# A hybrid attention and linear-attention step on one core: how far VectorE, ScalarE and GpSimd run in written order through layer 1

## The chip, the cores and the metric

The kernel runs on one core of a Trainium2 chip. The metric is the device time of one execution in microseconds (us). Before the change the median of three runs is 2579.01 us, from 2577.28 to 2580.81.

## What is computed

The reference runs two layers on 512 prompt rows and on 8 sequences of 16 sample rows, 640 rows in all, with a model width of 2048, in float32. Layer 0 is stick-breaking attention. Layer 1, where the change lies, is gated linear attention (GLA). Cut to what matters here:

```python
shift, scale, gate = jnp.split(c @ w_ada[i] + b_ada[i], 3, axis=-1)
h = rmsnorm(x, norm_g[i]) * (1 + scale[:, None]) + shift[:, None]
...
q, k, v, r, a_lr = jnp.split(h @ w_in, [nk, 2 * nk, 2 * nk + nv, 2 * nk + 2 * nv], axis=-1)
g = (jax.nn.log_sigmoid((a_lr @ w_a2 + b_a).astype(f32)) / GLA_TAU).reshape(B, T, GLA_HEADS, GLA_DK)
...
S, o = lax.scan(gla_chunk, S0, (to_chunks(q), to_chunks(k), to_chunks(v), to_chunks(g)))
...
y = (o.reshape(B, T, nv) * jax.nn.silu(r.astype(f32))).astype(h.dtype) @ w_out
```

The product `h @ w_in` gives queries, keys, values and gates for four heads, and `w_a2` is a small matrix (16 rows) that the decay gate needs later.

## The kernel before

**Numbers in two parts.** TensorE multiplies in a rounded float32 form, so each operand is held as a high part and a low part. `halves` (lines 133 to 135) makes them: ScalarE rounds the operand (line 134, CAST, named `wh` for weights), and VectorE subtracts that from the operand (line 135, `wl`). `split` (line 139) does so for a piece of weights of 128 x 1024. The buffers for the parts of a weight piece come in a ring of three, two in the pool `wp` and every third one in a pool that is given for the time being (`ring3`).

**Seven products.** Most of `h @ w_in` of layer 1 is done in blocks of 256 columns by a scheme with seven products in place of eight (`by_sevens`, line 480). A block is called a job here. Each of its products, named P0 to P6 below, is 24 matmuls (line 541) of a 128 x 128 weight tile with 320 rows. The seven weight pieces of a job, W0 to W6 in the order of the products, are made from four quarters that are loaded (b11, b12 and b22 into the buffers `wb`, b21 into a buffer `wr`), by `weights` (line 499):

- W0 is b11 itself. Behind it VectorE makes t = b22 - b12 (line 507) and b12 - b11 (line 508).
- W1 is b11 + t (made by line 510). W2 is b21, and behind it b21 - b11 is made (line 513).
- W3 is t. W4, W5 and W6 are b12 - b11, b21 - b11 and b22.

`ready` (line 528) keeps three pieces ahead: at the start of product Pn the piece for two products later is split, ahead of Pn's own matmuls in the program. Where a product ends, ScalarE or VectorE takes its sum out of PSUM (lines 547, 554 and 561: the tiles `m`, `u` and `out`). `u` of P1 must be taken before P3 goes on in the same bank, and `u` of P3 before P5 does.

**Seventeen jobs.** Three hold keys and queries, six hold values (`keep_value`, line 1329), eight hold gates (`keep_gate`, line 1340: a sigmoid on ScalarE, line 1346, and a product on VectorE, line 1348, per half). A finished job of values is turned into rows while the next job runs: `as_rows` (line 613) transposes it on TensorE in three groups g0, g1 and g2 (line 623) as a side lane, which `Side` (line 270) starts by a count of TensorE time. After each group `halves` writes a high and a low part of `kr` out of PSUM, and SyncE stores each to the DRAM tensors `gv`. There is one buffer for the high part of `kr` and one for the low part, so that a group's conversion waits until the store of the group before it is done.

**What sets the order.** TensorE always runs in the order in which the program is written. The other engines' instructions are put in order by a scheduler that goes by its own times, except inside a `manual_schedule` block, where the named engines too run in written order. One such block (`in_order`, line 1245) opens at layer 0's output projection. It closes at line 1365, when the last sum of layer 1's activations (`adds`, line 1270) is made. SyncE, which issues the loads (line 71) and stores (line 74) here, stays with the scheduler. On the chip each engine works through its list from front to back.

**Around the place of the change.** Ahead of it, two plain products make the queries of head 0 (`queries`, line 1311, matmuls on line 596, their copies `pl` on line 1304 and their stores `gq`). `next(sevens)` at the 30th step of the queries makes W0, t and b12 - b11 of the first job. Then the pool `om` is closed, and six small loads bring `w_a2` (`wa2r`), ScalarE rounds it (line 1374), VectorE subtracts (line 1375) and SyncE stores the result (`wa_d`), which only the next stage reads. Then `drive(sevens)` (line 1377) runs all seventeen jobs, `side.finish()` what is left of the side lanes, and `h2.again` (line 1380) makes activation parts for the stage that follows.

Of the kernel before, what the change touches and what calls it, by code (L numbers as in the profile page):

```python
# [41 lines left out]
def hybrid_step_kernel(ctx: ExitStack, tc: tile.TileContext, A: dict, O: list):  # L42
# [296 lines left out]
    def drive(*gens):  # L339
        for g in gens:  # L340
            for _ in g:
                side.tick()
# [812 lines left out]
    with tc.tile_pool(name="o0", bufs=1, reuse_waits="tile") as po, ExitStack() as only_d:  # L1155
# [89 lines left out]
        in_order = ExitStack()  # L1245
# [116 lines left out]
                next(sevens)  # L1362
        for _ in adds:
            pass
        in_order.close()
        more.close()
        ring3["n"] = 2
        ring3["pool"] = only_d.enter_context(tc.tile_pool(name="w2", bufs=1, reuse_waits="tile"))
# [7 lines left out]
        store(wa2_d, wa2.bitcast(F32))  # L1376
        drive(sevens)
        side.finish()
        ring3["pool"] = None
        h2.again(1, wq)  # L1380
    s1_pool.close()
# [541 lines left out]
```

## Time and profile before

| what | value |
|---|---|
| median of three runs | 2579.01 us |
| profiled execution, its own time | 2576.39 us |
| span of the profiled execution | 2574.6 us |
| TensorE (PE) busy | 2444.2 us, 95% of the span |
| VectorE (DVE) busy | 1604.6 us, 62% |
| ScalarE (ACT) busy | 1019.7 us, 40% |
| GpSimd (POOL) busy | 231.4 us, 9% |
| mean granted TensorE clock | 0.979 of full speed |
| the seven products of layer 1 | 1622 to 2059 us of the span |

The profile is of one execution, which took 2576.39 us: 1.8 us beside its span, and 2.6 us under the median. PE stands for TensorE's matmuls, PEld for its weight loads, SPq, ACTq and POOLq for the queues that issue DMAs. In rows of the timeline stand the start, the duration, the engine, the line, the operation with its output and inputs, and in brackets how long the engine had been idle and what released it. A row with x2 or more holds several instructions.

### The profile page before, as it was taken

How to read it: one execution, taken by the hardware profiler on the slowest of the kernel's cores; microseconds unless marked ns; L12 is line 12 of the kernel's file. 1: busy time of each engine (PE TensorE's matmuls, PEld its weight loads, DVE VectorE, ACT ScalarE, POOL GpSimd, SP SyncE). 2: the span in 40 equal slices, each digit the busy share in tenths (PEclk: the TensorE clock that was granted, in tenths of full speed). 3: DMA queues.
4: the chain of work that ended last, by engine and by line, in shares of the span. 5: the costliest groups of instructions: out<-in, count | busy, mean ns of one | idle time of the engine just before them, and what ended most of it. 6: DMA issues, size and time to landing. Idle time of an engine off the chain costs nothing. (4 is left out here: it accounts for less than half of the span.)

```text
span 2574.6 us, 43617 instructions
## 1 busy us (share of the span) xinstructions
PE 2444.2 (95%) x17321; PEld 2147.2 (83%) x17321; DVE 1604.6 (62%) x2445; ACT 1019.7 (40%) x1820; POOL 231.4 (9%) x489
## 2 busy tenths in 40 slices
PE   6899999999999999999999979899999998989998
PEld 4589999989999988787777758899999997766776
DVE  4675655555566656666776665766666655666466
ACT  4342222222223335655443344333333364565133
POOL 1220000000000000000000050000000114334200
PEclk8899999999999999999999989999999999999999
DMA  9966666766663366666665853344444367777464
GB/s 337 320 212 218 217 204 219 228 216 192 207 199 118 116 209 207 228 213 222 214 226 170 252 188 123 88 114 130 126 124 118 112 221 249 240 250 230 164 230 148
DMA packets 452797, 502.05 MB, mean 195 GB/s; under 512 B 26090, under 2 KB 349810, under 8 KB 452466
## 3 DMA queue, kind: packets, MB, share of 16 engines
q1 hardware_dynamic: 433090, 442.11, 54.1%
q0 software_dynamic: 16048, 51.92, 6.0%
q10 hardware_dynamic: 3456, 5.24, 0.6%
q8 instruction: 136, 2.23, 0.4%
q14 instruction: 67, 0.55, 0.1%
HBM read 410.05 MB, written 89.13 MB: 194 GB/s over the span
## 5 line engine op out<-in xcount | busy, mean ns | idle before, releaser
L541 PE MATMUL ps_mm<-sums,wh 128*128 128x320 f32 x2880 | 644.0, 312 | 2.2 <-ACT wh L134 2.2
L541 PEld LDWEIGHTS ps_mm<-sums,wh 128*128 128x128 f32 x2880 | 481.2, 189 | 11.3 <-issue 7.4
L541 PE MATMUL ps_mm<-h,wh 128*128 128x320 f32 x2160 | 484.7, 312 | 5.7 <-DVE u L547 3.2
L541 PE MATMUL ps_mm<-sums,wl 128*128 128x320 f32 x1440 | 446.4, 310 | 1.5 <-DVE wl L135 1.5
L541 PEld LDWEIGHTS ps_mm<-h,wh 128*128 128x128 f32 x2160 | 360.3, 188 | 22.1 <-issue 14.5
L135 DVE TENSOR_TENSOR wl<-wr,wh 128x1024 fp32r<-128x1024 f32 x192 | 236.0, 1230 | 213.9 <-ACT wh L134 213.1
L134 ACT CAST wh<-wb 128x1024 fp32r<-128x1024 f32 x178 | 186.8, 1049 | 449.6 <-PE ps_mm L541 381.6
L541 PE MATMUL ps_mm<-h,wl 128*128 128x320 f32 x1080 | 334.5, 310 | 0.7 <-DVE wl L135 0.7
L134 ACT CAST wh<-wr 128x1024 fp32r<-128x1024 f32 x192 | 201.6, 1050 | 316.0 <-PE ps_mm L541 194.1
L541 PEld LDWEIGHTS ps_mm<-sums,wl 128*128 128x128 f32 x1440 | 271.6, 189 | 2.0 <-DVE wl L135 2.0
L135 DVE TENSOR_TENSOR wl<-wb,wh 128x1024 fp32r<-128x1024 f32 x178 | 217.6, 1222 | 63.0 <-ACT wh L134 62.5
L642 PE MATMUL ps_mm<-wh,ogh 128*128 128x512 f32 x460 | 201.8, 439 | 13.2 <-ACT ogh L134 7.5
L596 PE MATMUL ps_mm<-h,wh 128*128 128x320 f32 x896 | 208.0, 319 | 6.1 <-ACT wh L134 3.3
L541 PEld LDWEIGHTS ps_mm<-h,wl 128*128 128x128 f32 x1080 | 203.5, 188 | 1.0 <-DVE wl L135 1.0
L642 PE MATMUL ps_mm<-wh,ogl 128*128 128x512 f32 x460 | 182.8, 397 | 0.6 <-DVE ogl L135 0.4
L642 PE MATMUL ps_mm<-wl,ogh 128*128 128x512 f32 x460 | 182.1, 396 | 0.0
L596 PEld LDWEIGHTS ps_mm<-h,wh 128*128 128x128 f32 x896 | 151.1, 191 | 17.6 <-issue 7.0
L596 PE MATMUL ps_mm<-h,wl 128*128 128x320 f32 x448 | 139.9, 312 | 3.1 <-DVE wl L135 3.1
L642 PEld LDWEIGHTS ps_mm<-wh,ogh 128*128 128x128 f32 x460 | 87.9, 191 | 41.5 <-issue 14.8
L898 DVE TENSOR_TENSOR_SCAN k<-k,zero_c 128x544 f32<-128x544 f32 (+4 forms) x96 | 93.3, 976 | 29.6 <-ACT k L894 16.9
L470 PE MATMUL ps_mm<-wh,h 128*128 128x512 f32 x288 | 101.7, 418 | 6.8 <-ACT h L134 4.9
L642 PEld LDWEIGHTS ps_mm<-wh,ogl 128*128 128x128 f32 x460 | 87.4, 190 | 21.8 <-DVE ogl L135 1.8
(341 smaller groups left out, 3830.6 us busy)
## 6 DMA issues: line engine op xcount, KB each, us to landing
ar<-in_w_ada_dram SPq DMA_DIRECT2D x160, 512.0 KB
wb<-in_sb_w_in_dram SPq DMA_DIRECT2D x82, 512.0 KB
kc<-in_cache_sb_k_dram SPq DMA_DIRECT2D x64, 512.0 KB
vc<-in_cache_sb_v_dram SPq DMA_DIRECT2D x64, 512.0 KB
wb<-in_gla_w_in_dram SPq DMA_DIRECT2D x51, 512.0 KB
wr<-in_gla_w_in_dram SPq DMA_DIRECT2D x45, 512.0 KB
wr<-in_sb_w_in_dram SPq DMA_DIRECT2D x44, 512.0 KB
ar<-in_w_ada_dram SPq DMA_DIRECT2D x64, 256.0 KB
```

Of the source, the lines that this page charges most:

```text
L134: nc.scalar.copy(hi, x)
L135: dve.tensor_tensor(lo, x, hi.bitcast(F32), op=ALU.subtract)
L470: mm(acc[a], l, by(l, r[:, e, :]), start=j == 0 and e == 0 and first, stop=j == 7 and e == 1 and last)
L541: mm(acc, l[:, k, :], by(l[:, k, :], r), start=start and k == 0 and first, stop=k == 7 and last, skip_group_check=True)
L596: mm(acc[nt], l[:, k, :], by(l[:, k, :], r), start=k0 == 8 and k == 0 and first, stop=k0 == 0 and k == 7 and last)
L642: mm(acc, l, by(l, r[:, e, :]), start=i == 0 and e == 0 and first, stop=i == 1 and e == 1 and last)
L898: dve.tensor_tensor_scan(kr, kr, zeros[:, :w], 1.0, ALU.mult, ALU.add)
```

## The change

The end of the `in_order` block moves from ahead of the loads of `w_a2` to behind `side.finish()`. VectorE, ScalarE and GpSimd now run in written order through the conversion of `w_a2` and all seventeen jobs.

```diff
         for _ in adds:
             pass
-        in_order.close()
         more.close()
         ring3["n"] = 2
         ring3["pool"] = only_d.enter_context(tc.tile_pool(name="w2", bufs=1, reuse_waits="tile"))
...
         store(wa2_d, wa2.bitcast(F32))
         drive(sevens)
         side.finish()
+        in_order.close()
         ring3["pool"] = None
         h2.again(1, wq)
```

No instruction is added or removed. TensorE's order is the same in both kernels, GpSimd's differs only in six DMAs and conversions of the next stage, and the other engines' lists differ as follows.

ScalarE at the start of the first job. The names: `wh<-wb` is the rounding of W0 and then of W1, `wh<-wr` that of W2, `pl` the last copy of the queries, `wa` the rounding of `w_a2`.

```order
 L134 CAST sums<-sx 128x320 x2
 L134 CAST wh<-wb 128x1024
-L134 CAST wh<-wr 128x1024
 L1304 COPY pl<-ps_mm 128x320
-L134 CAST wh<-wb 128x1024
-L1374 CAST wa_17021<-wa2r 96x1024
+L1373 CAST wa_17020<-wa2r 96x1024
+L134 CAST wh<-wb 128x1024
+L134 CAST wh<-wr 128x1024
```

W2 went from ahead of the copy to behind W1, and the rounding of `w_a2` from behind W1 to ahead of it.

VectorE at the same place. `wl` is the low part of W0, then of W2 (`wr`) and W1 (`wb`); L507, L508, L510 and L513 are the sums of weight quarters.

```order
 L135 TENSOR_TENSOR wl<-wb,wh 128x1024
 L507 TENSOR_TENSOR t_17001<-wb 128x1024
-L135 TENSOR_TENSOR wl<-wr,wh 128x1024
-L508 TENSOR_TENSOR wb<-wb 128x1024
+L508 TENSOR_TENSOR wb<-wb 128x1024
+L1374 TENSOR_TENSOR wa_17020<-wa2r,wa_17020 32x1024
 L510 TENSOR_TENSOR wb<-t_17001,wb 128x1024
-L513 TENSOR_TENSOR wr<-wr,wb 128x1024
-L135 TENSOR_TENSOR wl<-wb,wh 128x1024
-L1375 TENSOR_TENSOR wa_17021<-wa2r,wa_17021 32x1024
+L135 TENSOR_TENSOR wl<-wb,wh 128x1024
+L135 TENSOR_TENSOR wl<-wr,wh 128x1024
```

The subtraction for `w_a2` (line 1375 before, 1374 now) now stands ahead of L510, which makes W1.

VectorE in a job that runs while the values of the job before it are turned into rows, before the change, from W3's low part (`wl<-t`) on; the three rows of `kr` are g0, g1 and g2, the two of `u` are the sums of P1 and P3.

```order
L135 TENSOR_TENSOR wl<-t_18130,wh 128x1024
L135 TENSOR_TENSOR kr<-ps_tp,kr 128x512
L547 TENSOR_TENSOR u<-ps_mm,m_18190 128x320
L135 TENSOR_TENSOR wl<-wb,wh 128x1024
L135 TENSOR_TENSOR kr<-ps_tp,kr 128x512
L135 TENSOR_TENSOR wl<-wr,wh 128x1024
L135 TENSOR_TENSOR kr<-ps_tp,kr 128x256
L507 TENSOR_TENSOR t_18384<-wb 128x1024
L547 TENSOR_TENSOR u<-ps_mm,m_18190 128x320
```

The same place in the changed kernel, from L513 on.

```order
L513 TENSOR_TENSOR wr<-wr,wb 128x1024
L135 TENSOR_TENSOR kr<-ps_tp,kr 128x512
L135 TENSOR_TENSOR wl<-t_18129,wh 128x1024
L135 TENSOR_TENSOR kr<-ps_tp,kr 128x512
L547 TENSOR_TENSOR u<-ps_mm,m_18189 128x320
L135 TENSOR_TENSOR kr<-ps_tp,kr 128x256
L135 TENSOR_TENSOR wl<-wb,wh 128x1024
L135 TENSOR_TENSOR wl<-wr,wh 128x1024
L547 TENSOR_TENSOR u<-ps_mm,m_18189 128x320
```

All three groups of `kr` now stand ahead of W4 (`wl<-wb`), g1 also ahead of the `u` of P1, and the t of the next job (L507) has gone to behind W0 of that job. ScalarE's list has the same pattern. On SyncE the load of b12 now stands between g0's two stores and the load of b21 behind them; before, b12 came ahead of both, b21 between them, and b22 ahead of g1's second store.

## The prediction

> **What bounds the kernel now.** I read the page first, then the windows of the stretch that the change reorders, then what TensorE waited for in it, and last the timelines of the engines at its start and in one job.
>
> The page's first line, and the windows view: time of each engine within a stretch of layer 1's seven products, with the granted clock behind POOL.
>
> ```profile
> span 2574.6 us, 43617 instructions
> ...
> 1620.00:1740.00 120.00, 115.50 (x764) 114.60 (x764) 77.45 (x81) 41.00 (x51) 0.00 (x0) 0.97 0.40 112
> 1740.00:1880.00 140.00, 137.06 (x939) 135.56 (x939) 90.11 (x102) 49.85 (x65) 0.00 (x0) 1.00 0.46 130
> 1880.00:2060.00 180.00, 179.32 (x1223) 179.09 (x1222) 124.69 (x136) 69.20 (x85) 7.58 (x20) 1.00 0.40 115
> ```
>
> TensorE is busy for 115.50 of 120 us, 137.06 of 140 and 179.32 of 180, VectorE for some two thirds of each. So TensorE is the bound, and an order of the other engines can win little more here than TensorE's idle time: 4.5, 2.9 and 0.7 us. It can lose more, by making TensorE wait. The waits view of TensorE over 1620 to 2095 us (total, times, longest) names what there is:
>
> ```profile
> PE ps_mm L541 <- ACT wh L134: 3.0, 2, 2.3
> PE ps_mm L541 <- DVE u L547: 2.7, 4, 0.9
> ```
>
> The first is at the start of the first job, the second in the jobs that turn values into rows.
>
> **The start of the first job.** TensorE's timeline around product P0, then ScalarE's, VectorE's and SyncE's.
>
> ```profile
> 1619.80 0.31 PE L596 MATMUL ps_mm<-h,wl 128*128 128x320 f32 x1
> 1622.42 0.56 PE L541 MATMUL ps_mm<-h,wh 128*128 128x320 f32 x2 [2.31 <-ACT wh L134]
> ...
> 1628.39 0.31 PE L541 MATMUL ps_mm<-h,wl 128*128 128x320 f32 x1
> 1629.42 0.55 PE L541 MATMUL ps_mm<-sums,wh 128*128 128x320 f32 x2 [0.72 <-ACT wh L134]
> ```
> ```profile
> 1621.32 1.05 ACT L134 CAST wh<-wb 128x1024 fp32r<-128x1024 f32 x1
> 1622.27 1.05 ACT L134 CAST wh<-wr 128x1024 fp32r<-128x1024 f32 x1
> 1623.21 0.42 ACT L1304 COPY pl<-ps_mm 128x320 f32<-128x320 f32 x1
> 1628.32 1.05 ACT L134 CAST wh<-wb 128x1024 fp32r<-128x1024 f32 x1 [4.69 <-DVE wb L510]
> 1630.66 1.05 ACT L1374 CAST wa<-wa2r 96x1024 fp32r<-96x1024 f32 x1 [1.29 <-DMA wa2r<-in_gla_w_a_dram]
> ```
> ```profile
> 1624.67 1.22 DVE L135 TENSOR_TENSOR wl<-wr,wh 128x1024 fp32r<-128x1024 f32 x1
> 1625.81 1.22 DVE L508 TENSOR_TENSOR wb<-wb 128x1024 f32<-128x1024 f32 x1
> 1627.06 1.23 DVE L510 TENSOR_TENSOR wb<-t,wb 128x1024 f32<-128x1024 f32 x1
> ...
> 1631.74 1.22 DVE L1375 TENSOR_TENSOR wa<-wa2r,wa 32x1024 fp32r<-32x1024 f32 x1 [1.06 <-ACT wa L1374]
> ```
> ```profile
> 1606.73 17.26 SPq L74 DMA_DIRECT2D gq<-pl  x2
> 1625.98 2.65 SPq L71 DMA_DIRECT2D wa2r<-in_gla_w_a_dram  x6
> ```
>
> P0 ends at 1628.70 (1628.39 + 0.31). P1 begins at 1629.42, 1.10 after ScalarE took up W1 (1628.32), which came 0.03 behind L510 (1627.06 + 1.23). ScalarE met the small loads `wa2r` at 1630.66, and they were what it waited for: they had landed just then. That wait held up nothing, since W1 stood ahead of it. Now it stands ahead of W1 on both engines, and behind it are queued L510, W1, W2 and L513, for which P1 and P2 wait.
>
> Step by step. The copy `pl` moves up one CAST, from 1623.21 to 1622.26 (its sums were done at 1620.11), and with it the second store of `gq`. SyncE's loads of `wa2r` come behind it; I move them by the same 0.95, from 1625.98 to 1625.03, and their landing from 1630.66 to 1629.71. The CAST of `w_a2` takes 1.05, to 1630.76. The subtraction starts at 1630.79, and L510 follows 1.14 later (as L508 followed `wl`, 1624.67 to 1625.81), at 1631.93, and ends at 1633.16. W1 is taken up at 1633.19 and P1 begins 1.10 later, at 1634.29, against 1629.42: **+4.9 us**. TensorE stands still for 5.6 us, and nothing else is in its list there. If the loads land no earlier than before, it is +5.8. The last of the six is issued 2.65 behind the first, at 1627.7, so that they cannot land 2 us sooner than I have them: not below +2.9.
>
> P1 also meets the clock. The same windows view, with the clock behind POOL's 0.00:
>
> ```profile
> 1624.50:1628.00 3.50, 3.50 (x17) 3.50 (x16) 3.47 (x4) 0.00 (x0) 0.00 (x0) 0.54 0.43 142
> 1628.00:1631.40 3.40, 1.92 (x10) 1.40 (x10) 2.65 (x3) 1.79 (x2) 0.00 (x0) 0.97 0.29 65
> 1631.50:1635.00 3.50, 3.50 (x16) 3.50 (x15) 2.44 (x2) 1.47 (x3) 0.00 (x0) 0.52 0.88 239
> ```
>
> Behind each idle spell some 3.5 us run at half clock, which costs 1.7 us; behind the half-idle stretch 1628.0 to 1631.4 it is already paid once. I expect one such stretch for P1 as before, so 0, from -0.4 (part of it falls into the longer pause) to +1.7 (two of them). The Trainium skill, TensorE: Matmul & The Clock Gate, section "What's actually happening", says that after an idle window of about 3.4 us the array runs at half clock until it has been busy for such a window. By it the longer pause is followed by a half-clock stretch of its own, and if the window in which P1 starts again is not counted as busy the sum is 1.7 us higher. The clock of 0.52 behind the stretch that was idle for under half of it shows that less than a whole idle window is enough here.
>
> **The six jobs beside which values are turned into rows.** Their length now: the start of P5 in the last job before them and in the last of them; two sums of P1 one plain job apart; and the transposes of g0 and g2 in one job.
>
> ```profile
> 1720.09 0.46 PE L541 MATMUL ps_mm<-h,wh 128*128 128x320 f32 x2
> ...
> 1878.81 0.54 PE L541 MATMUL ps_mm<-h,wh 128*128 128x320 f32 x2 [0.87 <-DVE u L547]
> ```
> ```profile
> 1660.52 0.49 DVE L547 TENSOR_TENSOR u<-ps_mm,m 128x320 f32<-128x320 f32 x1 [1.38 <-PE ps_mm L541]
> 1685.16 0.49 DVE L547 TENSOR_TENSOR u<-ps_mm,m 128x320 f32<-128x320 f32 x1 [1.38 <-PE ps_mm L541]
> ```
> ```profile
> 1756.96 0.60 PE L623 MATMUL ps_tp<-ident,out 128*128 128x128 f32 x4
> 1761.36 0.38 PE L623 MATMUL ps_tp<-ident,out 128*128 128x128 f32 x2
> ```
>
> A plain job takes 24.64 us, so a product 3.52. From g0 to g2 lie one product and eight transposes, 4.40 us: 0.88 for eight, 1.10 for a job's ten. Six jobs without a wait would take 6 x 25.74 = 154.4; they took 158.7. So 4.3 us are lost now (a little over the idle 2.9, since a matmul's modelled end hides the first part of a gap), at P5, which waits for the `u` of P3 behind g2 and t. By the new order that wait goes (t stands behind W0). What is late next shows in the conversions and stores of one job:
>
> ```profile
> 1758.34 0.59 ACT L134 CAST kr<-ps_tp 128x512 fp32r<-128x512 f32 x1
> 1762.38 0.59 ACT L134 CAST kr<-ps_tp 128x512 fp32r<-128x512 f32 x1 [3.45 <-DMA gv<-kr]
> ```
> ```profile
> 1759.29 0.68 DVE L135 TENSOR_TENSOR kr<-ps_tp,kr 128x512 fp32r<-128x512 f32 x1
> 1765.51 0.69 DVE L135 TENSOR_TENSOR kr<-ps_tp,kr 128x512 fp32r<-128x512 f32 x1 [0.33 <-DMA gv<-kr]
> 1771.07 0.43 DVE L135 TENSOR_TENSOR kr<-ps_tp,kr 128x256 fp32r<-128x256 f32 x1 [2.13 <-DMA gv<-kr]
> ```
> ```profile
> 1758.95 0.37 SPq L74 DMA_DIRECT2D gv<-kr  x1
> 1759.41 0.42 SPq L71 DMA_DIRECT2D wr<-in_gla_w_in_dram  x1
> 1760.00 3.35 SPq L74 DMA_DIRECT2D gv<-kr  x2
> ```
>
> A store with no load just ahead of it frees its buffer in 3.4 us (1758.95 to 1762.38); one 0.6 us behind a 512 KB load takes 5.5 (1760.00 to 1765.51). In the new order, on this job's clock: g0's low part is stored at 1759.25, 0.4 behind the load of b12, so g1's low part begins at about 1764.6, ends at 1765.3, and the `u` of P1 at 1765.8. P2 begins 0.22 after g2, at 1761.58, and P3 would begin at 1765.10: 0.85 late. g1's high part (1762.3) is stored behind the load of b21, so g2's can be written at 1767.6; ScalarE takes up W4 behind it, at 1767.9, and VectorE, behind g2's low part, ends W4 at 1770.2. P4 begins at 1769.5 and asks for the low part 0.3 later: 0.5 late. With loads in the queue ending half a microsecond sooner the two come to 1.0, so I take 1.2 per job, 7.2 for six, against 4.3 now: **+2.9 us**. Were both stores free in 3.4 us, no wait would be left, and the term is -4.3. A low store took at most 6.7 us in these jobs (issue and next use):
>
> ```profile
> 1865.65 3.32 SPq L74 DMA_DIRECT2D gv<-kr  x2
> ...
> 1872.32 0.69 DVE L135 TENSOR_TENSOR kr<-ps_tp,kr 128x512 fp32r<-128x512 f32 x1 [1.55 <-DMA gv<-kr]
> ```
>
> With that at both places a job loses 2.4, and the term is +10.
>
> **The rest.** The three jobs of keys and queries and the eight of gates have no stores in the way of a conversion. Each piece is split two products (7.0 us) ahead, and CAST and subtraction take 2.3; VectorE's load is 124.69 of 180 us. Even with t, L508 and L510 in one turn (3 x 1.23) a piece is ready in time: 0. At the end the first gate half's product goes behind the last sum, so its store is some 2 us later and the last upper activation parts 0.5 to 1 later, while TensorE has other products: +0.3. Behind 2095 us a few conversions change places by one, each 1.05 to 1.23 long: 0, within 2 either way.
>
> **Sum.** 4.9 + 0 + 2.9 + 0 + 0.3 = 8.1 us on the profiled execution's 2576.39, so 2584.5; the median of the runs lies 2.6 above it, and on its 2579.0 I forecast **2587 us**.
>
> **Rivals.**
>
> - *The stores decide the other way.* If the engines take the stores ahead of the loads' remainder, the buffers are free in 3.4 us and the 4.3 us of waits go: 4.9 - 4.3 + 0.3, 2580. For it speaks that SyncE issues g0's high store ahead of the load now; against, the 5.5 us of each store directly behind a load. Chance 0.16.
> - *The small loads are early* (the side where it is not slower). If `wa2r` lands by 1625.9, the end of an L508 that has moved up by one subtraction, its conversion fills that subtraction's place (1.14) and P1 begins where it did: 0 at the start, and with the -4.3 of free stores and 0.3, 2575. It decides at 3.8 us sooner than my 1629.71. Against it stands the first issue at 1625.98. Chance 0.05, mostly short of 0.2%.
> - *Late stores pile up.* W4 late in every value job, +10 there, and a second half-clock stretch: 4.9 + 1.7 + 10, 2596. For it speaks the 6.7 us store; against, that it was one of six. Chance 0.09.
> - *The forecast*, 2584 to 2592: chance 0.70.
>
> **Numbers.** A measurement of this kernel can tell about 0.2% (5.2 us) from no change. Slower by more: the forecast, the piled-up case and the upper part of the first rival, 0.79. Within it 0.18, faster 0.03. The range runs from 2580.5, a little over the free stores, to 2595, short of the piled-up case; it leaves out under 2 in 10.
>
> **What would show it.** In the profile of the changed kernel: P1's first matmul at 1634 with over 5 us idle, released by ScalarE's `wh`; the CAST of `w_a2` at 1629.7 ahead of W1's; no wait of P5 for `u` in the value jobs, but one of P3 for `u` and of P4 for `wl`; none in the gate jobs. The prediction is wrong if P1 begins within 2 us of 1629.4, or if the six value jobs take under 154.5 or over 165 us.

## The result, and the profile after

The changed kernel takes 2588.54 us (median of 20 runs, 2580.16 to 2593.11), the kernel before 2578.93 (20 runs, 2574.48 to 2583.93). The ratio is 1.0034, with a 95% interval from 1.0026 to 1.0042: slower by 6.7 to 10.8 us. The profiled execution of the changed kernel took 2580.16 us, the lowest of its runs, so that its stages are compared with those of the kernel before, and not its total.

The page's first line and the windows view over the stretch of the seven products:

```profile
span 2578.4 us, 43568 instructions
...
1620.00:1740.00 120.00, 111.49 (x744) 110.55 (x745) 73.36 (x74) 37.65 (x45) 0.00 (x0) 0.97 0.38 105
1740.00:1880.00 140.00, 135.32 (x928) 133.83 (x927) 88.13 (x100) 49.00 (x65) 0.00 (x0) 1.00 0.47 132
1880.00:2065.00 185.00, 184.32 (x1257) 184.09 (x1256) 128.55 (x139) 70.81 (x87) 8.16 (x21) 1.00 0.40 116
```

The page counts 49 instructions fewer than before; they are semaphore instructions, and each engine's own count of work is the same. TensorE is now idle for 8.5 us in the first of these stretches (4.5 before), for 4.7 in the second (2.9) and for 0.7 in the third (0.7). The waits view of TensorE from 1615 to 2062 us (total, times, longest) says for what:

```profile
PE ps_mm L541 <- ACT wh L134: 9.5, 2, 7.2
PE ps_mm L541 <- DVE u L547: 4.7, 6, 1.8
PE ps_mm L541 <- DVE wl L135: 1.1, 2, 0.7
```

The first row has grown from 3.0 to 9.5 and the second from 2.7 to 4.7. These are the two places of the prediction.

**The start of the first job**, in the timelines of TensorE, ScalarE, VectorE and SyncE:

```profile
1620.30 0.56 PE L541 MATMUL ps_mm<-h,wh 128*128 128x320 f32 x2 [2.31 <-ACT wh L134]
1621.56 0.42 PE L541 MATMUL ps_mm<-h,wl 128*128 128x320 f32 x1 [0.70 <-DVE wl L135]
1632.20 0.90 PE L541 MATMUL ps_mm<-sums,wh 128*128 128x320 f32 x2 [7.15 <-ACT wh L134]
1633.46 0.64 PE L541 MATMUL ps_mm<-sums,wl 128*128 128x320 f32 x1 [0.36 <-DVE wl L135]
```
```profile
1620.15 0.42 ACT L1304 COPY pl<-ps_mm 128x320 f32<-128x320 f32 x1
1627.52 1.04 ACT L1373 CAST wa<-wa2r 96x1024 fp32r<-96x1024 f32 x1 [6.95 <-DMA wa2r<-in_gla_w_a_dram]
1631.11 1.04 ACT L134 CAST wh<-wb 128x1024 fp32r<-128x1024 f32 x1 [2.54 <-DVE wb L510]
```
```profile
1622.67 1.22 DVE L508 TENSOR_TENSOR wb<-wb 128x1024 f32<-128x1024 f32 x1
1628.60 1.22 DVE L1374 TENSOR_TENSOR wa<-wa2r,wa 32x1024 fp32r<-32x1024 f32 x1 [4.70 <-ACT wa L1373]
1629.85 1.23 DVE L510 TENSOR_TENSOR wb<-t,wb 128x1024 f32<-128x1024 f32 x1
```
```profile
1622.91 2.65 SPq L71 DMA_DIRECT2D wa2r<-in_gla_w_a_dram  x6
```

Three engines stand still for six small loads. ScalarE waits 6.95 us for `wa2r`, since the rounding of `w_a2` is next in its list, VectorE 4.70 us for ScalarE, and TensorE 7.15 us for W1, which ScalarE can only round once VectorE has made it (L510). The loads land 1.96 us behind the end of their last issue (1622.91 + 2.65, to 1627.52).

**A value job**, the second of the six, in VectorE's, ScalarE's, SyncE's and TensorE's timelines:

```profile
1767.82 0.69 DVE L135 TENSOR_TENSOR kr<-ps_tp,kr 128x512 fp32r<-128x512 f32 x1 [3.99 <-DMA gv<-kr]
1768.43 0.48 DVE L547 TENSOR_TENSOR u<-ps_mm,m 128x320 f32<-128x320 f32 x1
...
1771.31 1.23 DVE L135 TENSOR_TENSOR wl<-wb,wh 128x1024 fp32r<-128x1024 f32 x1
```
```profile
1764.21 0.59 ACT L134 CAST kr<-ps_tp 128x512 fp32r<-128x512 f32 x1 [1.63 <-DMA gv<-kr]
1769.96 0.37 ACT L134 CAST kr<-ps_tp 128x256 fp32r<-128x256 f32 x1 [5.16 <-DMA gv<-kr]
```
```profile
1761.66 0.37 SPq L74 DMA_DIRECT2D gv<-kr  x1
1762.12 0.42 SPq L71 DMA_DIRECT2D wb<-in_gla_w_in_dram  x1
1762.63 0.67 SPq L74 DMA_DIRECT2D gv<-kr  x1
1763.86 0.37 SPq L71 DMA_DIRECT2D wr<-in_gla_w_in_dram  x1
1764.82 6.72 SPq L74 DMA_DIRECT2D gv<-kr  x4
```
```profile
1769.06 0.53 PE L541 MATMUL ps_mm<-sums,wh 128*128 128x320 f32 x2 [0.34 <-DVE u L547]
...
1772.64 0.46 PE L541 MATMUL ps_mm<-sums,wh 128*128 128x320 f32 x2
```

g0's low part is stored at 1762.63, 0.5 us behind the load of b12, and its buffer comes free at 1767.82, 5.2 us later. VectorE waits 3.99 us of this with g1, and the `u` of P1 stands behind g1: it starts at 1768.43, and P3 with it. g1's high part, stored at 1764.82 behind the load of b21, frees its buffer 5.1 us later, at 1769.96. The last row is P4's start.

The six jobs do not lose alike. From P5 to P5 they take 27.05, 26.32, 26.35, 26.71, 26.28 and 27.80 us, where 25.74 would be without a wait. The sixth, in VectorE's and TensorE's timelines:

```profile
1874.96 0.69 DVE L135 TENSOR_TENSOR kr<-ps_tp,kr 128x512 fp32r<-128x512 f32 x1 [5.47 <-DMA gv<-kr]
```
```profile
1876.19 0.53 PE L541 MATMUL ps_mm<-sums,wh 128*128 128x320 f32 x2 [1.84 <-DVE u L547]
```

Its g0's low part, stored at 1868.28, frees the buffer only 6.7 us later. In the five profiles of kernels that run all value jobs in written order with the one buffer, this store takes 5.9 to 6.9 us in the first and the sixth job and 5.1 to 5.7 in the four between. In the first and the sixth, and in no other, a 16 KB load of instructions (queue 8 in the DMA view) starts 3.3 to 4.2 us behind the store. Whether it is what holds the store up was not tested.

### The profile page after: what moved, and what is told of

It is laid out like the page before. It is cut to its first block, busy times and chain, and to the rows that moved or that the text cites. A ratio compares the mean times of both kernels' runs of the same rounds, so it can differ in the third digit from the quotient of the medians.

```text
span 2578.4 us, 43568 instructions
## 1 busy us (share of the span) xinstructions
PE 2443.2 (95%) x17321; PEld 2146.4 (83%) x17321; DVE 1604.0 (62%) x2445; ACT 1020.1 (40%) x1820; POOL 229.8 (9%) x489
```

## The experiments

The first table takes from each profile the time from P0's first matmul to P1's; from there to the `u` of P1; the six value jobs with the job that hands over to the gates (`u` of P1 in the fourth job to that in the eleventh); and P0's first matmul to the first of the next stage (line 596). Without a wait the fourth column would be 6 x 25.74 + 24.64 = 179.1 us, by the durations in the prediction. The three jobs ahead of it last 73.9 to 74.0 us and what is behind it 165.95 to 166.01 us in every profile.

| kernel | P0 to P1 | P1 to its `u` | value jobs | all seven products |
|---|---|---|---|---|
| before | 7.00 | 6.46 | 183.43 | 436.81 |
| before, second profile | 7.12 | 4.81 | 182.80 | 434.65 |
| after | 11.90 | 6.32 | 185.25 | 443.36 |
| after, second profile | 11.92 | 6.54 | 185.71 | 444.05 |
| after, third profile | 11.93 | 6.72 | 185.98 | 444.51 |
| `first_job` | 11.87 | 6.50 | 183.15 | 441.52 |
| `wa2_later` | 5.99 | 4.79 | 185.67 | 436.33 |
| `wa2_later_kr2` | 5.99 | 4.80 | 179.19 | 429.84 |
| `after_kr2` | 11.88 | 6.03 | 179.17 | 436.96 |
| `after_kr2_b` | 11.95 | 6.49 | 179.16 | 437.49 |
| `before_kr2` | 7.22 | 4.70 | 179.33 | 431.17 |
| `loads_twice` | 16.23 | 6.31 | 185.90 | 448.33 |
| `kr2_n26` | 6.92 | 6.33 | 179.17 | 432.30 |
| `kr2_n22` | 5.64 | 5.80 | 179.17 | 430.49 |

The second table has the times, each beside the kernel before on the same chip. The last column is the first table's seven products less the mean of the two profiles of before, 435.7.

| kernel | median us (runs) | before | ratio, 95% interval | by the profile |
|---|---|---|---|---|
| after, again | 2585.01 (12) | 2576.30 | 1.0040, 1.0025 to 1.0055 | +8.3 |
| `first_job` | 2580.54 (12) | 2576.30 | 1.0012, 0.9995 to 1.0028 | +5.8 |
| `wa2_later` | 2577.43 (12) | 2576.30 | 1.0000, 0.9984 to 1.0017 | +0.6 |
| `wa2_later_kr2` | 2570.97 (12) | 2576.30 | 0.9981, 0.9962 to 0.9999 | -5.9 |
| `loads_twice` | 2586.92 (5) | 2574.24 | 1.0046, 1.0034 to 1.0059 | +12.6 |
| `before_kr2` | 2571.54 (12) | 2574.24 | 0.9987, 0.9975 to 1.0000 | -4.6 |
| `kr2_n26` | 2570.63 (12) | 2574.24 | 0.9982, 0.9970 to 0.9994 | -3.4 |
| `kr2_n22` | 2570.74 (12) | 2574.24 | 0.9991, 0.9978 to 1.0005 | -5.2 |
| `after_kr2` | 2580.56 (12) | 2573.43 | 1.0030, 1.0017 to 1.0043 | +1.2 |
| `after_kr2_b` | 2579.63 (12) | 2576.55 | 1.0010, 0.9996 to 1.0024 | +1.8 |

### The changed kernel again

> The changed kernel itself once more, for a second trace and a paired time. Start theory (the loads of w_a2 hold up W1 of the first job): P1 begins 11.9 us behind P0's start again (7.0 before), and the six value jobs lose some 6 us (4.3 before); the ratio is 1.0034, about 2588 us. If the first trace was an accident, P1 begins elsewhere. Clock theory: the part of the 9.6 us that the two traces do not show (some 3 us) is half-clock stretches, and this trace shows more of them between 1620 and 1645 than the first.

No edit. The loss is there in a second measurement, with a ratio of 1.0040, and the two parts in the trace have nearly the same size (11.92 and 185.71 us). As the clock theory had it, this trace has more half clock around P0 and P1 than the first, 13.7 us against 6.8 in the trace's record of the granted clock. But here it fell on P0 too, which took 7.3 us in place of 4.8 and only shortened the pause behind it, to 4.65 us from 7.15: P1 came no later, and the seven products last 0.7 us longer. So the clock at P0 does not explain the rest of the 9.6 us.

### The value part alone: the conversion of w_a2 later

> The whole of layer 1's products in written order, but the conversion of w_a2 is written 30 us of TensorE time later, behind the sum of the second job's P1 or so. Start theory: the 4.9 us at P1 go, and with W2's conversion out of the way P1 begins up to 0.7 us sooner than before the change; what is left is the value jobs' 1 to 3 us: 2580 to 2582, ratio 1.0005 to 1.001. Rival, that written order in the seventeen jobs themselves costs the time: it stays at 2586 to 2588.

```diff
-        nc.scalar.copy(wa2, r)
-        dve.tensor_tensor(wa2[64:96, :], r[64:96, :], wa2[64:96, :].bitcast(F32), op=ALU.subtract)
-        store(wa2_d, wa2.bitcast(F32))
+        def low_rank():
+            nc.scalar.copy(wa2, r)
+            dve.tensor_tensor(wa2[64:96, :], r[64:96, :], wa2[64:96, :].bitcast(F32), op=ALU.subtract)
+            store(wa2_d, wa2.bitcast(F32))
+
+        side.after(30.0, low_rank)
```

The written order stays to the end of the sevens, but the two conversions and the store of `w_a2` are written 30 us of TensorE's time further on. TensorE's timeline at P1, and ScalarE's at W1 and at the conversion:

```profile
1630.27 0.56 PE L541 MATMUL ps_mm<-sums,wh 128*128 128x320 f32 x2 [1.24 <-ACT wh L134]
```
```profile
1629.17 1.04 ACT L134 CAST wh<-wb 128x1024 fp32r<-128x1024 f32 x1 [4.62 <-DVE wb L510]
...
1657.46 1.05 ACT L1375 CAST wa<-wa2r 96x1024 fp32r<-96x1024 f32 x1
```

P1 now comes 5.99 us behind P0, and the conversion waits for nothing. The whole of the start's loss goes with this one step, and 1.07 us more than that against the 7.06 of the kernel before: in written order W2's low part (1.22 us) no longer stands ahead of L508 and L510 on VectorE. The value jobs keep their loss (185.67), and the time is that of the kernel before.

### The start alone: the written order only through the first job

> The written order ends behind the first job, so that the conversion of w_a2 stands ahead of W1 and all value and gate jobs have the scheduler's order. Start theory: +4.9 us at P1 and nothing else, about 2584, ratio 1.002; the value jobs wait at P5 for u as before, 2.7 us in the waits view. Rival, that the jobs' order costs the time: 2579.

```diff
-        drive(sevens)
+        for n, _ in enumerate(sevens):
+            side.tick()
+            if n == 13:
+                in_order.close()
         side.finish()
-        in_order.close()
```

From the second job on the scheduler orders the engines as in the kernel before. The start is late as in the changed kernel (11.87), the value jobs are at 183.15 us, and the ratio lies between those of before and after. Its interval holds 1 as well as the expected 1.002, so that the time alone does not tell the two theories apart; the trace does. In TensorE's waits from 1615 to 2062 us the start's part is still there, and the value jobs' part is back at the 2.7 us of before:

```profile
PE ps_mm L541 <- ACT wh L134: 7.0, 2, 4.7
PE ps_mm L541 <- DVE u L547: 2.7, 3, 1.7
```

### A second buffer for kr, in three kernels

In `wa2_later_kr2` it is added to `wa2_later`, in `before_kr2` to the kernel before, and in `after_kr2` and `after_kr2_b` (one kernel, measured twice) to the changed kernel. g1 takes the two tiles that held `w_a2`; g0 and g2 share the old pair.

```diff
-                    parts = [slot(12 + d, (P, 2, 256), name="kr")[:, :m, :] for d in range(2)]
+                    parts = [wa_in.tile([P, 2, 256], F32R, tag=("wa2r", "wa2")[d], name="kr") if g == 1 else
+                             slot(12 + d, (P, 2, 256), name="kr") for d in range(2)]
+                    parts = [t[:, :m, :] for t in parts]
```

> As with w_a2 converted later, and the middle group of value rows has buffers of its own (those of w_a2, which are free by then), so that no group waits for the store of the one just before it. Store theory (the value jobs lose their time to the stores that free the one buffer): the waits of P3 for u go, 4.3 us less than before in the six jobs and about 1 less at the start: 2573 to 2575, ratio 0.998. Rival, that VectorE simply has too much ahead of u: the waits stay and the time is that of the kernel without the second buffer, 2580 to 2582.

> The kernel before, in the scheduler's order, with a second buffer for the high and the low part of kr. If the one buffer, which is free only when a store has landed, makes the waits of the value jobs in the kernel before too, these fall from 183.4 to about 179.1 us, and the time by 4.3 us (ratio 0.9983). If they come from the order in which the scheduler puts the u of P3 behind g2 and t, the jobs stay over 182 us and the time within 1.5 us of before.

> The changed kernel with a second buffer for kr and nothing else. If the two parts of the loss are independent, the start keeps its 11.9 us from P0 to P1, the value jobs fall to about 179.2 us, the sevens last 437 us (about as in the kernel before), and the time is 1 us over the kernel before (ratio 1.0003), some 7 us under the changed kernel. If the value jobs of the changed order wait for something besides the stores, they stay over 182 us and the ratio over 1.0015.

> The changed kernel with a second buffer for kr, measured once more: in its first measurement the sevens lasted 437.0 us, 1.2 us over the mean of the two profiles of the kernel before, while the ratio was 1.0030. If the sevens' time is the whole difference, the ratio now comes out between 0.9995 and 1.0015. If the pause at the start also costs something outside the sevens (a lower clock later), it is 1.0020 or more again, with a mean granted clock of the runs 0.001 or more under that of the kernel before, and the sevens are at 437 us again.

VectorE's timeline in a value job of `wa2_later_kr2`, and then TensorE's waits from 1615 to 2062 us:

```profile
1758.66 0.69 DVE L135 TENSOR_TENSOR kr<-ps_tp,kr 128x512 fp32r<-128x512 f32 x1
1759.81 0.49 DVE L547 TENSOR_TENSOR u<-ps_mm,m 128x320 f32<-128x320 f32 x1 [0.45 <-PE ps_mm L541]
1763.68 0.43 DVE L135 TENSOR_TENSOR kr<-ps_tp,kr 128x256 fp32r<-128x256 f32 x1 [3.38 <-DMA gv<-kr]
```
```profile
PE ps_mm L541 <- ACT wh L134: 2.0, 2, 1.2
PE ps_mm L541 <- DVE wl L135: 1.4, 2, 0.7
```

g1 no longer waits for a store, `u` follows P1 in time, and the wait for `kr` has moved to g2, behind which W4's low part stands and not `u`. TensorE's waits for `u` are gone. The value jobs fall to 179.2 us whatever the order: in written order with `w_a2` late, in written order with `w_a2` early, and in the scheduler's (179.33). So the waits of the kernel before at P5 had the same root, the one buffer. With both edits, `wa2_later_kr2` is faster than both kernels: 0.9981 of the kernel before, 0.9962 to 0.9999.

`after_kr2` keeps the late start and has no loss in the value jobs, so its seven products come to 437.0 and 437.5 us, 1.2 and 1.8 over before. Its two ratios are 1.0030 and 1.0010. The second agrees with the trace; the first lies above it by more than its interval. The mean granted clock of the runs is below that of the kernel before in both, 0.9766 against 0.9792 and 0.9779 against 0.9789, as the theory of a cost outside the sevens had it. Among the twelve runs of the first measurement 0.001 less goes with some 1.9 us more, so that by an estimate the 0.0026 are worth some 5 us. Of the lower clock, the longer half-clock spells at P0 and P1 (10.2 and 13.7 us in the two traces, 6.8 in both of before) make about 0.0007 and 0.0013, by an estimate; where the rest of the first one's comes from isn't shown. That there is a further cost of the late start outside the sevens can't be excluded by these two runs.

### The dose at the start: each small load twice

> The changed kernel, but each of the six small loads of w_a2 is issued twice, so that the last one leaves SyncE 2.65 us later. If the start of P1 hangs on the landing of these loads, as the prediction has it, P1 follows P0 by about 14.5 us in place of 11.9, the sevens last 2.6 us longer than in the changed kernel, and the time is some 11 us over the kernel before (ratio 1.0042). If P1 is late because of the two conversions that stand ahead of it, whenever their input comes, it stays at 11.9 us, with a ratio of 1.0033.

```diff
             load(r[16 * n:16 * n + 16, :], A["gla_w_a2"][0])
+            load(r[16 * n:16 * n + 16, :], A["gla_w_a2"][0])
```

SyncE's, ScalarE's and TensorE's timelines:

```profile
1625.77 6.95 SPq L71 DMA_DIRECT2D wa2r<-in_gla_w_a_dram  x12
```
```profile
1634.71 1.04 ACT L1374 CAST wa<-wa2r 96x1024 fp32r<-96x1024 f32 x1 [11.28 <-DMA wa2r<-in_gla_w_a_dram]
```
```profile
1639.39 0.90 PE L541 MATMUL ps_mm<-sums,wh 128*128 128x320 f32 x2 [8.80 <-ACT wh L134]
```

Twelve loads took 6.95 us to issue where six took 2.65, which is 4.30 more and not 2.65 as expected. P1 moved by the same: 16.23 us behind P0, 4.33 more than 11.90. The landing is 1.99 us behind the end of the issues (1.96 with six loads), and from it to P1 there are 4.68 us in both kernels. So the start follows the landing one for one; the two conversions add a fixed part behind it.

### W0 earlier

> The version with the conversion of w_a2 later and a second buffer for kr, and besides W0, t and b12 - b11 of the first job made at the 26th step of the queries in place of the 30th. If W0's rounding comes late for P0 only because it is written late (TensorE waits 2.3 us for it before), that wait falls to under 0.5 us and the time is 2 us below the version without this step, some 7 under the kernel before (ratio 0.9973). If it comes late because the last sums stand ahead of it or its own load lands late, it stays within 0.5 us of that version (ratio 0.9981).

> As the run with the 26th step, at the 22nd step. If the wait for W0 goes with earlier writing, the time is that of the 26th step, about 7 us under the kernel before (ratio 0.9973). If the three operations of VectorE (3.7 us) now hold back the sums that stand behind them, and the queries wait for these, it is slower than with the 26th step by up to 3 us.

```diff
-            if n == 30:
+            if n == 26:
                 next(sevens)
```

Both on top of `wa2_later_kr2`; the other run has 22. TensorE's timeline of the run with 26 at P1, then VectorE's ahead of it:

```profile
1625.62 0.56 PE L541 MATMUL ps_mm<-sums,wh 128*128 128x320 f32 x2 [2.72 <-ACT wh L134]
```
```profile
1620.52 1.22 DVE L508 TENSOR_TENSOR wb<-wb 128x1024 f32<-128x1024 f32 x1
1621.66 1.69 DVE L135 TENSOR_TENSOR sums<-sx,sums 128x320 fp32r<-128x320 f32 x4
1623.27 1.22 DVE L510 TENSOR_TENSOR wb<-t,wb 128x1024 f32<-128x1024 f32 x1
```

P0 now follows the last product of the queries without a pause (2.3 us before), as the first theory had it, but its 2 us were not won: W1 didn't move up with it. L510 stands behind the last sums on VectorE, so P1 waits 2.72 us where it waited 1.25, and meets half clock besides (6.33 us to its `u`). By the profiles 3.4 us in the sevens and P0's 2.3 ahead of them are saved against the kernel before, 5.7 in all, as without the step (5.9). The ratio too is that of the version without it, 0.9982 beside 0.9981. At the 22nd step P1's wait is 1.95 us; 0.9991 with an interval from 0.9978 to 1.0005 doesn't tell it from either.

### Two more profiles

> The kernel before, once more, for a second profile. The question is what the start of the sevens and the stages behind them do from run to run. If the stages behind the sevens vary from run to run and not by kernel, their 515.4 us here may come out anywhere between 508 and 517 us, and the sevens again at 436.8 us, within 2.5 by the clock at their start.

> The changed kernel, a third profile. If the loss is all in the sevens, these last 443 to 444.5 us again, and the stages behind them lie in the same spread as those of the kernel before (508 to 517 us). If the changed order also costs 2 to 3 us behind the sevens, they are at 517 us or more.

These single runs took 2572.76 us (the kernel before) and 2585.38 (the changed one). From the first matmul behind the sevens to the end of the span lie 515.4 and 516.1 us in the two profiles of before, and 514.7, 513.9 and 517.1 in the three of after: one of the three reaches the 517 us that the second theory named, but their mean, 515.2, is below that of before, 515.8. Over all fourteen profiles it is 508.2 to 518.1. P0 itself begins between 1620.2 and 1631.3 us in the twelve profiles whose W0 is written at the 30th step. So the stages on both sides of the sevens vary from run to run by more than can be laid to the change, and the loss that shows is in the sevens.

## Why the prediction was right

**The start, +4.9.** P1 was to begin 11.87 us behind P0 (1634.29 less 1622.42); it does so after 11.90, 11.92 and 11.93, against 7.00 and 7.12 before: +4.9. The chain holds at each step: counted from P0, `w_a2` was to be taken up at 7.29, L510 at 9.51 and W1 at 10.77; they come at 7.22, 9.55 and 10.81. P0 itself began 2.1 us earlier than in the profile of before, so the distances from P0 answer to the prediction's times, not the times themselves. `wa2_later` shows the cause by taking it away, and `loads_twice` by doubling the loads.

**The clock, 0 within -0.4 and +1.7.** For the pair of profiles on which the sum was made it is 0: P1 takes 6.32 us to its `u` after the change and 6.46 before. But that was a chance of the first profile. The second one of before has 4.81, as have the runs whose P1 waited only 1.24 us. The windows view of the changed kernel around the pause, then that of `wa2_later` over the same two products (the clock is behind POOL's 0.00):

```profile
1625.00:1630.00 5.00, 0.05 (x1) 0.00 (x0) 1.37 (x2) 1.04 (x1) 0.00 (x0) 1.00 0.14 40
1630.00:1634.00 4.00, 1.44 (x4) 1.04 (x5) 2.89 (x3) 2.89 (x4) 0.00 (x0) 0.51 0.34 98
1634.00:1637.50 3.50, 3.50 (x17) 3.50 (x16) 2.91 (x3) 0.37 (x1) 0.00 (x0) 0.59 0.09 17
```
```profile
1627.20:1630.20 3.00, 1.83 (x13) 1.56 (x11) 1.90 (x2) 1.03 (x2) 0.00 (x0) 1.00 0.36 112
1630.20:1635.00 4.80, 4.04 (x25) 3.77 (x26) 4.72 (x4) 2.33 (x5) 0.00 (x0) 1.00 0.04 12
```

In all nine profiles in which TensorE stood still for 1.95 us or more ahead of P1, P1 was slow and took 5.80 to 6.72 us to its `u`; of the five with 1.25 us or less (two of them none at all) only one did, and the other four took 4.70 to 4.81. So over the profiles the change costs 0.9 us here: a mean of 6.53 after against 5.64 before. With two profiles of before that are 1.65 us apart this is a rough figure. The Trainium skill, TensorE: Matmul & The Clock Gate, section "What's actually happening", has the activity window run free of the kernel's start and gives about 3.4 us for an idle one. By that it would count where in a window a pause falls, and the one in five agrees, as does the half clock behind each of the long pauses. But the pause of 1.95 us, behind which P1 was slow too, is well short of an idle window, and there the measurement decides.

**The six value jobs, +2.9.** Measured: 185.25, 185.71 and 185.98 us against 183.43 and 182.80, +2.5 in the means. By the prediction's own measure, P5 to P5, the six take 160.5 us. The mechanism at P3 was right: g1's low part waits for a store that follows a load (5.2 us in the job shown; the prediction had 5.5), `u` stands behind it, and P3 waits. P5's wait is gone as forecast. One step failed: "P4 begins at 1769.5 and asks for the low part 0.3 later: 0.5 late". P4 never waited. Both waits for `wl` in the after profile, 0.70 and 0.36, are in the first job. In the job shown W4's low part is ready at 1772.54 (1771.31 + 1.23), 3.5 us behind P3's start, and P4 begins at 1772.64; the prediction had 4.25 us from P3's start (1770.2 less 1765.95, its 1765.10 + 0.85). It had g1's high part stored 3.05 us behind g0's low one (1762.3 less 1759.25), and the trace has 2.19 (1764.82 less 1762.63), so that g2 and W4 could follow sooner: g0's high store, with nothing issued in the 12 us ahead of it, was free after 2.6 us (1761.66 to 1764.21), where the prediction counts 3.4. P3's own wait was near the 0.85 of the prediction in the four jobs in the middle, which lose 0.5 to 1.1 us each in the three profiles, but the first and the sixth lose 1.3 to 2.3 behind their longer stores. So the mean of 1.0 to 1.15 us per job came near the 1.2 by luck: two long stores stand where P4's wait was put. The term was 0.4 too high.

**The rest, +0.3.** The plain jobs have the same 73.92 us. From the last value job to the next stage it is 165.97 after and 166.00 before: 0. Behind that no difference stands out of the spread.

**The sum.** 4.9 + 0.9 + 2.5 + 0 is 8.3 us, and the profiles' totals differ by 8.2 (443.97 less 435.73 in the means), where 8.1 was forecast. That the sum fits so well is luck in part, since the clock's 0.9 too little offsets the 0.4 and 0.3 too much. The medians differ by 9.6 and 8.7 us. The forecast of 2587 us is 1.5 below the median.

**The rivals.** The stores did not decide the other way: value jobs under 179.5 us come only with a second buffer. The small loads were not early, since the conversion took up at 7.22 us behind P0. Late stores did not pile up in every job: only the first and the sixth come near that rival's 2.4 us. Its 6.7 us store was the one of the sixth job, and this job's is long again in each profile of after.

**What stays open.** The first measurement of `after_kr2` is some 6 us above what its trace shows (7.1 between the medians, 1.2 in the sevens), and its repetition is not. The lower granted clock of that measurement goes with most of the excess, but why it was lower was not settled. Nor was what makes the store long in the first and the sixth value job.

## What to carry to other kernels

An engine stops at the first instruction of its list whose data aren't there, here ScalarE for 6.95 us, so before a written order is drawn further, look through the stretch for instructions that wait for a transfer issued shortly before, and write them where the transfer has long landed. Here one conversion, whose result nobody reads for 400 us, cost 4.9 us, and moving it gave all of that back. Where the order of two kernels differs and both lose time in the same place, look for a resource behind both: a second buffer was worth 3.8 us in one order and 6.5 in the other. And take away a wait only after asking what stands behind it: P0's 2.3 us came back at P1.

## What the runs showed of the hardware

Twelve loads of 16 rows each took SyncE 6.95 us to issue where six took 2.65, more than twice as much, while each time the last one landed 2.0 us behind the end of the issues. A 256 KB store 0.5 us behind a 512 KB load freed its buffer after 5.1 to 5.7 us in the middle jobs of the five profiles, and after 5.9 to 6.9 in the two jobs where a load of instructions began meanwhile; a store 1.8 us behind such a load took 3.4 in the profile before (1758.95 to 1762.38), and one with nothing issued in the 12 us ahead of it 2.6 in that of after (1761.66 to 1764.21). And TensorE's half clock depends on more than the length of a pause: ahead of P1 it followed each of nine pauses of 1.95 to 8.80 us and one of five shorter or absent ones, but behind P0's own pause of 2.31 us it came in the profile before (0.54 from 1624.5 us on) and not in that of the changed kernel, in the windows view of P0:

```profile
1620.00:1623.50 3.50, 2.50 (x15) 2.24 (x16) 3.19 (x3) 0.57 (x2) 0.00 (x0) 1.00 0.25 96
1623.50:1625.20 1.70, 1.55 (x11) 1.29 (x9) 0.40 (x1) 0.00 (x0) 0.00 (x0) 1.00 0.46 116
```

In the clock records of the fourteen traces, each half-clock spell that begins with P0 or in the 11 us behind it lasts 3.41, 6.83 or 10.24 us. The two profiles of the kernel before differ by 1.65 us from P1 to its `u` alone.
